# A hybrid retention and attention layer: the MLP norm's weight applied per channel block, a fixed order in the first q and k panels, and the embedding's products in the other PSUM pool

## The chip, the cores and the metric

The kernel runs on one core of a Trainium2 chip. The metric is the device time of one execution in microseconds (us), as the median of several runs. The engines of the core work side by side, each through its own queue in order: TensorE (PE) multiplies, VectorE (DVE) and ScalarE (ACT) work on tiles, GpSimd (POOL) does a few small things, SyncE (SP) starts most transfers. Products are added up in PSUM, in banks of 128 partitions x 512 numbers (fp32); everything else lies in SBUF.

## The reference

One layer on 512 tokens (S) of 1024 channels (D); everything is fp32. The MLP has 4096 hidden channels. What matters here:

```
rmsnorm(x, g) = x * rsqrt(mean(x*x) + eps) * g
h  = rmsnorm(x, g_mix);  z = h @ w_in        # retention q, k, v, gate; attention q, k, v; merge gates
x  = x + (sig(gA) * (A @ w_ret_out) + sig(gB) * (B @ w_att_out)) @ w_o
x  = x + relu(rmsnorm(x, g_mlp) @ w_up)**2 @ w_down
x  = x + sig(rmsnorm(x, g_ple) @ w_ple_gate) * (p @ w_ple_proj)
```

A is the retention, B the attention of three groups of four heads, whose q and k are normed per head and rotated (rotary).

## The kernel before, in words

**Products.** Each fp32 operand is split into a high part, rounded to the matmul's type, and a low part, the rest. A product is three matmuls (mm3, L235 to L241): high x high, high x low, low x high, each of 128x128 by 128x512. A piece of weights (raw, 256 rows x 512 columns, 512 KB) is fetched through SP and split by split_unit: whi by a copy on ACT (L227), wlo by a subtraction on DVE (L228). `ahead` and `AHEAD` set how many pieces are split before they are used. There are two PSUM pools of four banks: psg (names pg) and psa (names pt, pa, pb, ph and others).

**Turning.** The operand that a product contracts over must lie with channels on the partitions. split_T (L308) turns a half of a token tile (128 tokens x 512 channels) by four transposes on PE (L315) into one bank, and then makes the high and low parts from the bank. Without a weight this is one copy on ACT (L328) and one subtraction on DVE (L329), 128x512 each. With a weight (gcol) it is done for each of the four 128-channel blocks: the channel is now the partition, so that the weight is a scale of one number per partition in ACT's copy (L323) and in DVE's combined multiply and subtract (L324). The retention's output is turned in this way.

**Start (setup, first_panel).** setup starts the transfers on SP in order: the columns of x and of the first weights by turns (L390, L391), x by tokens (L397, 4 x 512 KB), then the rotation tables and gains (load_tables), then the next weights. A table of weights per channel, gcol (40 columns), comes through ACT's queue (L382). PE does WARM = 10 matmuls on zeros (L408). first_panel (L438) multiplies the q columns of attention group 0; its scaling and splitting is pinned into a fixed order. token_factors (L502) squares x by tokens on ACT (L508) and makes the norm's factors. For each of four token tiles att_proj squares the product per head (L578), makes a factor on DVE (L579) and POOL (L580), rotates (four operations on DVE, L531 to L536, with the tables C and S of L560), and scales (L585). Then follows the k panel in the same manner with rows_gemm.

**w_o and the embedding (tail).** The product with w_o is one level of Strassen-like recursion with seven products (seven_gemm, L943). Its sums go from PSUM into x on DVE (acc, L967); one pair of sums passes through a tile m (copied by ACT, L981, added to on DVE, L995). Whenever a half of a token tile of x is complete, `ready` (in tail) calls gain_T (L357): a multiplication with g_mlp as a row table gr on DVE (L362), then, some steps later, split_T without a weight into h2h and h2l, the operand of w_up. `later` and `tick` place such steps between products: the lag is a number of ticks. mean_squares (L366) squares x on ACT for the MLP norm's factors, with the lag 3 + 2j. Then embed (L490) multiplies p with w_ple_proj: 8 banks of 6 matmuls, copied out by ACT and DVE in turns (L145, L149) and stored. Its banks are psg's, in which seven_gemm also has the sums that are still to be added to x. seven_gemm and embed are under manual_schedule for ACT and DVE: their order on these two is that of the code. PE's order is made by a scheduler.

Of the kernel before, what the change touches and what calls it, by code (L numbers as in the profile page):

```python
# [31 lines left out]
WARM = 10  # L32
# [43 lines left out]
class Block:  # L76
# [140 lines left out]
    def split_unit(self, raw, g0):  # L217

        nc = self.nc
        k = raw.shape[1]  # L220
        hi = self.wsp.tile([P, 1024], F32, tag="whi", name=self.nm("whi")).rearrange("p (k n) -> p k n", k=k)
        lo = self.wsp.tile([P, 1024], F32, tag="wlo", name=self.nm("wlo")).rearrange("p (k n) -> p k n", k=k)
        if g0 is None:
            for i in range(k) if self.pinned else [slice(0, k)]:
                if self.hook is not None:
                    self.hook(i)
                self.pin(nc.scalar.activation(R(hi[:, i]), raw[:, i], AF.Copy))  # L227
                nc.vector.tensor_tensor(R(lo[:, i]), raw[:, i], hi[:, i], op=ALU.subtract)  # L228
# [14 lines left out]
    def rows_gemm(self, act, nk, consume, perm=False, group=2, need=None, halves=False):  # L243
# [3 lines left out]
        for u0 in range(0, nu, group):  # L247
            us = self.units(min(group, nu - u0))
            for t in range(NT):
                if need is not None:  # L250
                    need(t, u0)
                if u0 == 0:
                    banks[t] = self.gbank()
# [54 lines left out]
    def split_T(self, src, t, gcol, c, dst, bank=None):  # L308

        nc = self.nc  # L310
        for part in src:
# [4 lines left out]
            for k in range(n):  # L316
# [6 lines left out]
                nc.scalar.activation(R(hi), i, AF.Copy, scale=g)  # L323
# [24 lines left out]
    def gain_row(self, name):  # L348
        out = []
        for h in range(2):  # L350
            g = self.a[name][0]
            t = self.tabp.tile([P, 512], F32, tag="tab", name=self.nm("gr"))
            self.nc.sync.dma_start(t, bass.AP(tensor=g.tensor, offset=g.offset + 512 * h, ap=[[0, P], [1, 512]]))
            out.append(t)
        return out

    def gain_T(self, x, t, h, gain, dst, key, lag, bank=None):  # L357

        y = x[:, h * 512 : (h + 1) * 512]
        if gain is not None:  # L360
            y = self.tmp("y")
            self.nc.vector.tensor_tensor(y, x[:, h * 512 : (h + 1) * 512], gain[h], op=ALU.mult)  # L362
        self.later(lag, lambda: self.split_T([y], t, None, 4 * h, dst, bank), (key, t, h))
# [15 lines left out]
    def setup(self):  # L379
        nc, a = self.nc, self.a  # L380
        self.gcol = self.const.tile([P, 40], F32, name="gcol")
        nc.scalar.dma_start(self.gcol, a["vec_cols"])  # L382
# [16 lines left out]
        self.load_tables()  # L399
# [38 lines left out]
    def first_panel(self, consume):  # L438
# [23 lines left out]
        for k in range(KD // 2):  # L462
            for t in range(NT):
                part(t, k)
        self.pinned = True
        self.token_factors()
        self.pinned = False
        for t in range(NT):
# [3 lines left out]
            if t == 0:  # L472
# [17 lines left out]
    def embed(self):  # L490
# [3 lines left out]
        for half in range(2):  # L494
# [5 lines left out]
            self.rows_gemm(([hi], [lo]), 2, store)  # L500

    def token_factors(self):  # L502

        nc = self.nc
        ss = self.small(NT, "ss")
        for t in range(NT):
            j = self.big("j").rearrange("p a b -> p (a b)")[:, :D] if t == 0 else j
            self.pin(nc.scalar.activation(j, self.x_tiles[t], AF.Square, accum_out=ss[:, t : t + 1]))  # L508
# [58 lines left out]
    def att_proj(self, g, n):  # L567
# [3 lines left out]
        rots = []  # L571

        def consume(t, ps):
            ss, v, r = self.small(H, "ss"), self.small(H, "v"), self.small(H, "r")
            j = self.tmp("j")
            for h in range(H):
                c = slice(h * HD, (h + 1) * HD)
                nc.scalar.activation(j[:, c], ps[:, c], AF.Square, accum_out=ss[:, h : h + 1])  # L578
            nc.vector.tensor_scalar(v, ss, 1.0 / HD, self.floor[:, t : t + 1], op0=ALU.mult, op1=ALU.add)  # L579
            nc.gpsimd.tensor_tensor(r, v, self.mhalf[:, :H], op=ALU.pow)  # L580
            if not tabs:
                tabs.append(self.tables(g, n))
            C, Sn = tabs[0]
            o = self.rotate(ps, C[:, t], Sn[:, t])
            nc.vector.tensor_tensor(o.rearrange("p (h e) -> p h e", h=H), o.rearrange("p (h e) -> p h e", h=H),  # L585
                                    r.unsqueeze(2).to_broadcast([P, H, HD]), op=ALU.mult)
            rots.append(o)

        if lazy:
            self.first_panel(consume)  # L590
# [34 lines left out]
    def attention(self, g):  # L625
        nc = self.nc
        qT = self.att_proj(g, 0)
        if g == 0:
            self.load_rest()
        kT = self.att_proj(g, 1)  # L630
# [380 lines left out]
    def tail(self, mx):  # L1011
        nc, a = self.nc, self.a
        xs = self.xs
        g2 = self.gain_row("g_mlp")
# [11 lines left out]
        def ready(t, j, free):  # L1026
# [3 lines left out]
            self.gain_T(xs[t], t, j, g2, h2, "h2", 2 * j if late else 1 + t // 2,  # L1030
                        None if late else (lambda s: free) if t < 2 else self.gbank)
# [16 lines left out]
        for f in range(NF // 2):  # L1048
# [21 lines left out]
            if f == NF // 2 - 1:  # L1070
# [3 lines left out]
                def ready(t, j, free):  # L1074
                    late = (t < 2) == (j == 0)
                    self.gain_T(xs[t], t, j, None, h3, "h3", 0 if late else 1 + t // 2,
# [69 lines left out]
_INS = ["x", "w_in", "g_mlp", "w_ret_out", "w_att_out", "w_o", "w_up", "w_down", "w_ple_proj", "w_ple_gate"]  # L1146
# [25 lines left out]
```

## Time and profile before

| | us |
|---|---|
| Three runs | 1007.2, 1004.25, 1005.76 |
| Median | 1005.76 |
| The profiled execution | 1004.37 |
| Its span in the trace | 1002.5 |
| Between the two | 1.9 |
| PE busy | 990.5 |
| DVE busy | 639.6 |
| ACT busy | 446.6 |

In rows of the trace stand the start in us from the span's start, the duration, the engine, the line, the operation, output<-inputs by the program's names, partitions x elements, and the count; in brackets the idle time ahead of it and what ended it. Consecutive instructions on an engine overlap by a tenth of a us or so, so that the time from start to start is shorter than the duration. In a table of groups, busy time and mean ns stand behind the first bar, and idle time ahead of the group and who ended it behind the second.

### The profile page before, as it was taken

What the parts mean: (1) busy time and instruction counts of PE and PEld (TensorE: products, weight loads), DVE (VectorE), ACT (ScalarE), POOL (GpSimd) and SP (SyncE); (2) the same over time, 40 slices, a digit from 0 to 9 for tenths busy, and PEclk for the clock granted to TensorE, in tenths of its full rate; (3) what the DMA queues carried; (4) which work ended last, traced back from release to release, by engine and by line L of the source; (5) the groups of instructions that cost most, each with busy time, mean ns of one, the idle gap of its engine ahead of it and who ended that gap; (6) DMA issues with size and microseconds to landing.
All of it is one profiled execution on the core that took longest, in us unless ns stands there. A gap on an engine that the chain in (4) does not pass through costs nothing.

```text
span 1002.5 us, 12321 instructions
## 1 busy us (share of the span) xinstructions
PE 990.5 (99%) x4607; PEld 826.8 (82%) x4607; DVE 639.6 (64%) x930; ACT 446.6 (45%) x845; POOL 91.7 (9%) x98
## 2 busy tenths in 40 slices
PE   9899999999999999999999998999999999999998
PEld 6788899889888888888888877888888888888886
DVE  5966675764779345554643698469468658656953
ACT  7435344443534325342422445564454356355451
POOL 1100110110000010001002010101101001010000
PEclk9999999999999999999999999999999999999999
DMA  9622122333254412222446496749748856884911
GB/s 347 241 84 68 61 84 84 106 96 94 66 162 123 122 45 85 85 82 87 133 145 163 128 211 190 207 109 238 190 114 212 222 155 152 226 178 118 313 54 53
DMA packets 89756, 141.14 MB, mean 141 GB/s; under 512 B 6320, under 2 KB 38368, under 8 KB 89696
## 3 DMA queue, kind: packets, MB, share of 16 engines
q1 hardware_dynamic: 78672, 119.36, 36.9%
q0 software_dynamic: 10880, 20.97, 12.5%
q8 instruction: 36, 0.59, 0.2%
q14 instruction: 24, 0.20, 0.1%
q10 hardware_dynamic: 144, 0.02, 0.0%
HBM read 136.09 MB, written 4.24 MB: 140 GB/s over the span
## 4 chain that ended last, share of the span: by engine, by line
PE 93%; DMA 3%; DVE 2%; ACT 1%; issue 1%; SPq 0%; ACTq 0%; DVEq 0%
PE pg L239 26%; PE pg L240 26%; PE pg L241 26%; PE pb L239 3%; PE pb L240 3%; PE pb L241 3%; DMA raw<-in_w_in 2%; PE po L666 1%; PE ph L546 1%; PE pt L315 1%; PE sc L643 1%; DMA x<-in_x 1%; PE ry L846 1%; PE pe L620 1%; PE kv L834 1%
## 5 line engine op out<-in xcount | busy, mean ns | idle before, releaser
L228 DVE TENSOR_TENSOR wlo<-raw,whi 128x1024 fp32r<-128x1024 f32 (+1 forms) x198 | 235.8, 1195 | 119.1 <-ACT whi L227 117.3
L227 ACT ACTIVATE whi<-raw 128x1024 fp32r<-128x1024 f32 (+1 forms) x198 | 203.4, 1033 | 213.7 <-PE pg L241 84.9
L239 PE MATMUL pg<-whi,hh 128*128 128x512 f32 x480 | 198.8, 415 | 2.9 <-DVE ro L534 2.9
L240 PE MATMUL pg<-wlo,hh 128*128 128x512 f32 x480 | 188.1, 392 | 0.1
L241 PE MATMUL pg<-whi,hl 128*128 128x512 f32 x480 | 188.1, 392 | 0.0
L239 PEld LDWEIGHTS pg<-whi,hh 128*128 128x128 f32 x480 | 98.0, 204 | 17.9 <-issue 3.6
L241 PEld LDWEIGHTS pg<-whi,hl 128*128 128x128 f32 x480 | 97.9, 204 | 16.9
L240 PEld LDWEIGHTS pg<-wlo,hh 128*128 128x128 f32 x480 | 98.4, 205 | 14.6 <-DVE wlo L228 0.8
L239 PE MATMUL pg<-h2h,whi 128*128 128x512 f32 x256 | 99.6, 389 | 0.0
L240 PE MATMUL pg<-h2l,whi 128*128 128x512 f32 x256 | 99.6, 389 | 0.0
L241 PE MATMUL pg<-h2h,wlo 128*128 128x512 f32 x256 | 99.6, 389 | 0.0
L196 POOL DMA_DIRECT2D raw<-in_w_down x32 | 38.6, 1206 | 305.8 <-DMA raw<-in_w_down 220.7
L239 PE MATMUL pg<-whi,uh 128*128 128x512 f32 x160 | 62.7, 393 | 0.0
L241 PE MATMUL pg<-whi,ul 128*128 128x512 f32 x160 | 62.5, 392 | 0.0
L240 PE MATMUL pg<-wlo,uh 128*128 128x512 f32 x160 | 62.4, 390 | 0.0
L239 PEld LDWEIGHTS pg<-h2h,whi 128*128 128x128 f32 x256 | 48.0, 188 | 10.1
L241 PEld LDWEIGHTS pg<-h2h,wlo 128*128 128x128 f32 x256 | 48.0, 188 | 10.0
L240 PEld LDWEIGHTS pg<-h2l,whi 128*128 128x128 f32 x256 | 48.0, 188 | 9.9
L239 PE MATMUL pg<-hh,whi 128*128 128x512 f32 x128 | 52.4, 409 | 0.0
L940 DVE TENSOR_TENSOR ul<-z,uh 128x1792 fp32r<-128x1792 f32 x20 | 40.5, 2026 | 15.5 <-ACT uh L939 15.5
L241 PE MATMUL pg<-hh,wlo 128*128 128x512 f32 x128 | 50.0, 390 | 0.0
L240 PE MATMUL pg<-hl,whi 128*128 128x512 f32 x128 | 49.9, 390 | 0.0
(196 smaller groups left out, 1615.8 us busy)
## 6 DMA issues: line engine op xcount, KB each, us to landing
raw<-in_w_in SPq DMA_DIRECT2D x72, 512.0 KB, 3.9
raw<-in_w_down SPq DMA_DIRECT2D x48, 512.0 KB, 4.4
raw<-in_w_up SPq DMA_DIRECT2D x32, 512.0 KB, 5.4
raw<-in_w_down POOLq DMA_DIRECT2D x32, 512.0 KB, 6.0
raw<-in_w_o SPq DMA_DIRECT2D x12, 512.0 KB, 3.8
x<-in_x SPq DMA_DIRECT2D x8, 512.0 KB, 6.1
raw<-in_w_ret_out SPq DMA_DIRECT2D x8, 512.0 KB, 3.5
raw<-in_w_o POOLq DMA_DIRECT2D x8, 512.0 KB, 5.9
```

Of the source, the lines that this page charges most:

```text
L196: self.nc.gpsimd.dma_start(raw, rows(add[0]), accum_op=ALU.add)
L227: self.pin(nc.scalar.activation(R(hi[:, i]), raw[:, i], AF.Copy))
L228: nc.vector.tensor_tensor(R(lo[:, i]), raw[:, i], hi[:, i], op=ALU.subtract)
L239: t.matmul(ps, sh, mh, start=first, stop=False, skip_group_check=more)
L240: t.matmul(ps, sh, ml, start=False, stop=False, skip_group_check=more)
L241: t.matmul(ps, sl, mh, start=False, stop=last, skip_group_check=more)
L315: nc.tensor.transpose(ps[:, k * P : (k + 1) * P], part[:, k * P : (k + 1) * P], self.ident)
L546: self.nc.tensor.transpose(ps[:, t * P : (t + 1) * P], rots[t][:, h * HD : (h + 1) * HD], self.ident)
L620: self.nc.tensor.transpose(ps[:, k * P : (k + 1) * P], e[:, k * P : (k + 1) * P], self.ident)
L643: nc.tensor.matmul(sc[:, h * P : (h + 1) * P], qT[:, h, rs], kT[:, h, rs], start=True, stop=True)
L666: nc.tensor.matmul(po[:, h * P : (h + 1) * P], v[:, vt, h * HD : (h + 1) * HD], pt, start=b == 0, stop=b == len(blocks) - 1)
L940: nc.vector.tensor_tensor(R(lo), src, hi, op=ALU.subtract)
```

## The change

1. **g_mlp per channel.** gcol has 48 columns, the last eight with g_mlp. The row table gr, its two transfers and the multiplication L362 are gone; split_T gets the weight as gcol, and so does four ACT and four DVE operations of 128x128 for each of eight halves.
2. **Pool.** embed takes its banks from psa.
3. **Lag.** mean_squares has lag 9.
4. **First q and k panels.** They are under manual_schedule for ACT and DVE. The tables C and S are made ahead of the squares of x; a tile is rotated ahead of its factor and scaled one tile later; the next weights are split after tile 1 instead of tile 0.
5. **Start.** The tables' transfers stand ahead of x. The first half of the first weights goes through ACT's queue, ahead of gcol, and is split by a copy on DVE; the first twelve matmuls stand in another order; WARM is 7.

```
-WARM = 10
+WARM = 7
...
+                early = self.hook is not None and i == 0 and not self.loaded
+                if early:
+                    self.tc.keep_in_program_order(nc.vector.tensor_copy(R(hi[:, i]), raw[:, i]))
...
-    def gain_T(self, x, t, h, gain, dst, key, lag, bank=None):
-
-        y = x[:, h * 512 : (h + 1) * 512]
-        if gain is not None:
-            y = self.tmp("y")
-            self.nc.vector.tensor_tensor(y, x[:, h * 512 : (h + 1) * 512], gain[h], op=ALU.mult)
-        self.later(lag, lambda: self.split_T([y], t, None, 4 * h, dst, bank), (key, t, h))
+    def half_T(self, x, t, h, gain, dst, key, lag, bank=None):
+
+        self.later(lag, lambda: self.split_T([x[:, h * 512 : (h + 1) * 512]], t, gain, 4 * h, dst, bank), (key, t, h))
...
-                nc.sync.dma_start(raw[:, k], src[k * P : (k + 1) * P])
+                queue = nc.sync if u or k else nc.scalar
+                queue.dma_start(raw[:, k], src[k * P : (k + 1) * P])
+                if queue is nc.scalar:
+                    nc.scalar.dma_start(self.gcol, a["vec_cols"])
             self.raws.append((raw, None))
+        self.load_tables()
         self.x_tiles = []
...
-        self.load_tables()
         self.fetch(6)
...
-        for k in range(KD // 2):
+        (wh, wl), mm = us[0], nc.tensor.matmul
+        parts = [self.stat(self.hT, 0, t, False) for t in range(NT)]
+        for t, (sh, _) in enumerate(parts):
+            mm(banks[t], sh, wh[:, 0], start=True, stop=False)
+        for t, (_, sl) in enumerate(parts):
+            mm(banks[t], sl, wh[:, 0], start=False, stop=False)
+        for t, (sh, _) in enumerate(parts):
+            mm(banks[t], sh, wl[:, 0], start=False, stop=False)
+        for k in range(1, KD // 2):
             for t in range(NT):
                 part(t, k)
-        self.pinned = True
-        self.token_factors()
-        self.pinned = False
+        tables()
+        self.token_squares()
...
-            if t == 0:
+            if t == 1:
                 self.pinned = True
                 self.ahead(2)
...
-            self.rows_gemm(([hi], [lo]), 2, store)
+            self.rows_gemm(([hi], [lo]), 2, store, bank=self.bank)
...
+            C, Sn = tabs[0]
+            rots.append(self.rotate(ps, C[:, t], Sn[:, t]))
+            if lazy and t == 0:
+                self.token_factors()
             nc.vector.tensor_scalar(v, ss, 1.0 / HD, self.floor[:, t : t + 1], op0=ALU.mult, op1=ALU.add)
             nc.gpsimd.tensor_tensor(r, v, self.mhalf[:, :H], op=ALU.pow)
...
+            if t:
+                scale(t - 1)
+            factors.append(r)
+            if t == NT - 1:
+                scale(t)
...
-        g2 = self.gain_row("g_mlp")
+        g2 = lambda k: self.gcol[:, 40 + k : 41 + k]
...
-                self.later(3 + 2 * j, lambda: self.mean_squares(xs[t], v2[:, t : t + 1]), ("v2", t))
+                self.later(9, lambda: self.mean_squares(xs[t], v2[:, t : t + 1]), ("v2", t))
```

Line numbers move a little: whi and wlo are L231 and L232 after the change, the blocks L327 and L328, acc L980, the addition to m L1008, the rotation L535 to L540, the scale L597.

The order of the instructions, as the two programs have it, at three places. On DVE in the w_o product, before: x is the residual, y its product with the weight gr, wlo a weight's low part, h2l the low part of w_up's operand.

```order
L967 SCALAR_TENSOR_TENSOR x_4442<-pg_4800,one,x_4442 128x512
L967 SCALAR_TENSOR_TENSOR x_4442<-pb_4820,one,x_4442 128x512
L362 TENSOR_TENSOR y_4897<-x_4442,gr_4746 128x512
L228 TENSOR_TENSOR wlo_4900<-raw_4845,whi_4899 128x1024
L329 TENSOR_TENSOR h2l_4890<-pb_4881,h2h_4888 128x4x128
L329 TENSOR_TENSOR h2l_4890<-pb_4882,h2h_4888 128x4x128
L228 TENSOR_TENSOR wlo_4931<-raw_4927,whi_4930 128x1024
L967 SCALAR_TENSOR_TENSOR x_4443<-pg_4772,one,x_4443 128x512
L362 TENSOR_TENSOR y_4947<-x_4443,gr_4744 128x512
```

And after, with the same four sums into x ahead:

```order
L980 SCALAR_TENSOR_TENSOR x_4442<-pg_4789,one,x_4442 128x512
L980 SCALAR_TENSOR_TENSOR x_4442<-pb_4809,one,x_4442 128x512
L980 SCALAR_TENSOR_TENSOR x_4442<-pg_4796,one,x_4442 128x512
L980 SCALAR_TENSOR_TENSOR x_4442<-pb_4816,one,x_4442 128x512
L232 TENSOR_TENSOR wlo_4892<-raw_4841,whi_4891 128x1024
L328 SCALAR_TENSOR_TENSOR h2l_4886<-pb_4877,gcol,h2h_4884 128x128 x4
L328 SCALAR_TENSOR_TENSOR h2l_4886<-pb_4878,gcol,h2h_4884 128x128 x4
L232 TENSOR_TENSOR wlo_4935<-raw_4931,whi_4934 128x1024
L980 SCALAR_TENSOR_TENSOR x_4443<-pg_4768,one,x_4443 128x512 x2
L980 SCALAR_TENSOR_TENSOR x_4443<-pg_4775,one,x_4443 128x512
```

The multiplications are gone, and between the two wlo stand 2 x 4 blocks that read the banks pb and ACT's h2h in place of 2 operations. On ACT at the same place, before (m is the tile of one pair of sums, whi a weight's high part, pT the turned p):

```order
L981 ACTIVATE m_4883<-pg_4772 128x512
L981 ACTIVATE m_4893<-pg_4779 128x512
L227 ACTIVATE whi_4899<-raw_4845 128x1024
L328 ACTIVATE h2h_4888<-pb_4881 128x4x128
L328 ACTIVATE h2h_4888<-pb_4882 128x4x128
L227 ACTIVATE whi_4930<-raw_4927 128x1024
L487 ACTIVATE pT_4748<-praw_4749 128x1024
```

And after:

```order
L994 ACTIVATE m_4879<-pg_4768 128x512
L994 ACTIVATE m_4887<-pg_4775 128x512
L231 ACTIVATE whi_4891<-raw_4841 128x1024
L327 ACTIVATE h2h_4884<-pb_4877,gcol 128x128 x4
L327 ACTIVATE h2h_4884<-pb_4878,gcol 128x128 x4
L231 ACTIVATE whi_4934<-raw_4931 128x1024
L487 ACTIVATE pT_4744<-praw_4745 128x1024
```

The weights' high parts stand behind 4 or 8 blocks, where they stood behind 1 or 2 operations. On PE, the embedding's products with the turned p in after; the matmuls with h2h and h2l are w_up's first, and x is what is turned:

```order
L243 MATMUL pa_5140<-whi_5061,pT_4744 128x512
L244 MATMUL pa_5140<-wlo_5062,pT_4744 128x512
L245 MATMUL pa_5140<-whi_5061,pT_4744 128x512
L243 MATMUL pg_5285<-h2h_4883,whi_5126 128x512
L244 MATMUL pg_5285<-h2l_4885,whi_5126 128x512
L243 MATMUL pg_5286<-h2h_4883,whi_5126 128x512
L244 MATMUL pg_5286<-h2l_4885,whi_5126 128x512
L319 MATMUL pt_5150<-ident,x_4443 128x128 x4
L243 MATMUL pa_5163<-whi_5061,pT_4744 128x512
L244 MATMUL pa_5163<-wlo_5062,pT_4744 128x512
L245 MATMUL pa_5163<-whi_5061,pT_4744 128x512
L243 MATMUL pa_5163<-whi_5061,pT_4744 128x512
```

In before all 48 products of the embedding, in banks pg, stand ahead of w_up's first; now 36 of them stand behind w_up's first, which needs whi_5126 from ACT and the blocks of h2h and h2l.

On DVE in the head, before: ss are sums of squares, ro the rotated tiles, wlo_290 the first half of the k panel's weights.

```order
L511 TENSOR_SCALAR v_245<-ss_239 128x4
L513 TENSOR_SCALAR floor<-v_245 128x4
L579 TENSOR_SCALAR v_268<-ss_267,floor 128x4
L560 TENSOR_TENSOR C_277<-rotc_114,mg_115 128x512
L560 TENSOR_TENSOR S_278<-rotc_114,mg_115 128x512
L531 TENSOR_TENSOR ro_281<-pg_187,C_277 128x512
L534 TENSOR_TENSOR ro_282<-pg_187,S_278 128x4x64 x2
L228 TENSOR_TENSOR wlo_290<-raw_118,whi_289 128x512
L536 TENSOR_TENSOR ro_283<-ro_281,ro_282 128x512
L228 TENSOR_TENSOR wlo_290<-raw_118,whi_289 128x512
```

And after, where wlo_318 is that weight:

```order
L535 TENSOR_TENSOR ro_268<-pg_186,C_238 128x512
L538 TENSOR_TENSOR ro_269<-pg_186,S_239 128x4x64 x2
L540 TENSOR_TENSOR ro_270<-ro_268,ro_269 128x512
L515 TENSOR_SCALAR v_275<-ss_242 128x4
L517 TENSOR_SCALAR floor<-v_275 128x4
L587 TENSOR_SCALAR v_261<-ss_260,floor 128x4
L535 TENSOR_TENSOR ro_307<-pg_187,C_238 128x512
L538 TENSOR_TENSOR ro_308<-pg_187,S_239 128x4x64 x2
L540 TENSOR_TENSOR ro_309<-ro_307,ro_308 128x512
L587 TENSOR_SCALAR v_300<-ss_299,floor 128x4
L597 TENSOR_TENSOR ro_270<-ro_270,r_262 128x512
L232 TENSOR_TENSOR wlo_318<-raw_118,whi_317 128x512 x2
```

The first wlo of the k panel stood behind the first steps of one tile's rotation, and stands behind two whole tiles and one scale now; C and S stand ahead of these rows.

More of the change, by code (lines that the diff above doesn't have):

```diff
@@ L252, in rows_gemm @@
                 if u0 == 0:
-                    banks[t] = self.gbank()
+                    banks[t] = (bank or self.gbank)()
                 cols = [slice(0, 512)] if not (halves and t == NT - 1) else [slice(0, 256), slice(256, 512)]
@@ L380, in setup @@
         nc, a = self.nc, self.a
[L381 to L382 removed]
+        self.gcol = self.const.tile([P, 48], F32, name="gcol")
         xr = [self.big("xr") for _ in range(2)]
@@ L1143, in run @@
         assert self.used == len(self.plan) and not self.queue
-_INS = ["x", "w_in", "g_mlp", "w_ret_out", "w_att_out", "w_o", "w_up", "w_down", "w_ple_proj", "w_ple_gate"]
+_INS = ["x", "w_in", "w_ret_out", "w_att_out", "w_o", "w_up", "w_down", "w_ple_proj", "w_ple_gate"]
 def kernel(**inputs):
```

55 lines of the change are left out of this document (25 added, 30 removed).

## The prediction

> **What bounds the kernel now.** I read the page's first part, then the chain of waits of PE, then the two stretches that the change touches, the w_o product with the embedding (583 to 623 us) and the first panels (0 to 53 us). PE is the bound.
>
> ```profile
> span 1002.5 us, 12321 instructions
> PE 990.5 (99%) x4607; PEld 826.8 (82%) x4607; DVE 639.6 (64%) x930; ACT 446.6 (45%) x845; POOL 91.7 (9%) x98
> ```
>
> So only some 12 us of the span are not matmuls, and a change can gain no more than PE's waits. These are all of them that have a releaser:
>
> ```profile
> PE pg L239 <- DVE ro L534: 2.9, 1, 2.9
> PE pg L239 <- DVE x L967: 2.1, 1, 2.1
> PE warm L408 <- DVE warm L404: 1.5, 1, 1.5
> PE pg L240 <- DVE wlo L228: 0.5, 1, 0.5
> PE ph L546 <- DVE ro L536: 0.2, 1, 0.2
> ```
>
> Each is a wait for DVE. The first is in the head (at 34 us), the second and fourth are in the embedding's products. The places that the change touches hold these three, 5.5 us together. To lose is easier than to gain: an average of 64% hides that DVE is full just where the change adds work. In the table of windows the columns are length, then busy time and count of PE, PEld, DVE, ACT, POOL:
>
> ```profile
> 583.20:609.30 26.10, 25.51 (x122) 19.96 (x120) 25.58 (x35) 9.89 (x13) 2.42 (x2) 1.00 0.72 189
> 609.30:623.20 13.90, 11.80 (x55) 9.46 (x56) 12.33 (x21) 11.47 (x26) 0.00 (x0) 1.00 0.61 187
> ```
>
> In the w_o product DVE is busy 25.58 of 26.10 us and PE waits almost never: both are full. What is put into DVE's queue here, work or waiting, comes out at the end.
>
> **Part 1, the weight per channel block.** Groups of 583.2 to 624 us:
>
> ```profile
> L228 DVE TENSOR_TENSOR wlo<-raw,whi 128x1024 fp32r<-128x1024 f32 x11 | 13.4, 1220 | 0.1
> L362 DVE TENSOR_TENSOR y<-x,gr 128x512 f32<-128x512 f32 x8 | 5.5, 692 | 0.3
> L329 DVE TENSOR_TENSOR h2l<-pt,h2h 128x512 fp32r<-128x512 f32 x6 | 4.0, 682 | 0.0
> L329 DVE TENSOR_TENSOR h2l<-pb,h2h 128x512 fp32r<-128x512 f32 x2 | 1.3, 683 | 0.0
> ```
>
> Removed from DVE: 8 multiplies L362 (5.5 us) and 8 splits L329 (4.0 + 1.3), 10.8 us. Added: 32 blocks of 128x128 on ACT, then 32 on DVE. The same lines of split_T run in the retention, and show what such a block costs (timeline of ACT and of DVE):
>
> ```profile
> 382.10 0.37 ACT L323 ACTIVATE A<-pt,gcol 128x128 fp32r<-128x128 f32 x1 [0.46 <-PE pt L315]
> 382.89 0.37 ACT L323 ACTIVATE A<-pt,gcol 128x128 fp32r<-128x128 f32 x1 [0.42 <-DVE A L324]
> ...
> 390.93 0.61 ACT L323 ACTIVATE A<-pt,gcol 128x128 fp32r<-128x128 f32 x2
> ```
> ```profile
> 382.50 0.35 DVE L324 SCALAR_TENSOR_TENSOR A<-pt,gcol,A 128x128 fp32r<-128x128 f32 x1 [0.47 <-ACT A L323]
> 383.29 0.35 DVE L324 SCALAR_TENSOR_TENSOR A<-pt,gcol,A 128x128 fp32r<-128x128 f32 x1 [0.43 <-ACT A L323]
> ```
>
> By busy time it is even: 32 x 0.35 = 11.2 for 10.8. But DVE's block waits for ACT's, and ACT's second block of the same bank waits for DVE's first (0.42 <-DVE A L324). The period is 382.89 - 382.10 = 0.79 us, in which DVE works 0.35. Only blocks of two banks in turn go without that wait (0.61 for two, at 390.93), and the change issues the four blocks of a bank one after another. Four cost DVE 0.35 + 3 x 0.79 = 2.72 us where a split and a multiply cost 1.36, and the period holds ACT as well, where the next whi stands behind the blocks, and DVE's next wlo behind that whi. To price this I follow DVE's queue in its new order. The pitches, from rows of this stretch:
>
> ```profile
> 600.00 0.68 DVE L995 TENSOR_TENSOR m<-m,pb 128x512 f32<-128x512 f32 x1
> 600.71 1.42 DVE L967 SCALAR_TENSOR_TENSOR x<-m,one,x 128x512 f32<-128x512 f32 x2
> 602.04 0.68 DVE L995 TENSOR_TENSOR m<-m,pb 128x512 f32<-128x512 f32 x1
> ...
> 608.01 1.22 DVE L228 TENSOR_TENSOR wlo<-raw,whi 128x1024 fp32r<-128x1024 f32 x1
> 609.14 1.28 DVE L329 TENSOR_TENSOR h2l<-pt,h2h 128x512 fp32r<-128x512 f32 x2
> ```
> ```profile
> 598.13 2.00 ACT L227 ACTIVATE whi<-raw 128x1024 fp32r<-128x1024 f32 x2
> ```
>
> From start to next start an addition into x (acc, L967) takes 0.67, an addition to m 0.71, a wlo 1.13; a whi 0.95 on ACT. Time t runs from the first acc of the stage to the first matmul of w_up:
>
> ```profile
> 583.23 0.74 DVE L967 SCALAR_TENSOR_TENSOR x<-pg,one,x 128x512 f32<-128x512 f32 x1
> ...
> 623.16 0.39 PE L239 MATMUL pg<-h2h,whi 128*128 128x512 f32 x1
> ```
>
> This took 39.9 us. After the change, ends on DVE: 4 accs 2.7; wlo 3.8; four blocks 6.5 (3.8 + 2.72); four of the second bank 9.2; ACT, free at 8.9, makes the whi until 9.8, so that the wlo waits and ends at 10.9; 3 accs, the split of p (at wlo's pitch), an acc 14.7; wlo 15.9; four blocks 18.6; again a wlo behind the whi behind the blocks (18.3 + 0.95) 20.4; four blocks 23.1; 2 additions to m and 4 accs 27.2; wlo 28.3; 2 accs 29.7; wlo 30.8; eight blocks 36.2. ACT, held by the same eight until 35.9, makes two whi until 37.8, and the second one is for w_up, whose first products now stand among the embedding's: PE stops there until 37.9. From there PE has 36 of the embedding's 48 matmuls, 14 of w_up and 8 transposes before the place that answers to 623.16:
>
> ```profile
> 594.95 0.39 PE L239 MATMUL pb<-whi,uh 128*128 128x512 f32 x1
> ...
> 597.00 0.60 PE L315 MATMUL pt<-ident,y 128*128 128x128 f32 x4
> 597.36 0.48 PE L239 MATMUL pb<-whi,uh 128*128 128x512 f32 x1
> 597.67 0.39 PE L240 MATMUL pb<-wlo,uh 128*128 128x512 f32 x1
> ```
>
> Nine matmuls from 594.95 to 597.00 give 0.228 each; four transposes take 597.67 - 597.00 - 0.23 = 0.44. So 50 x 0.228 + 0.9 = 12.3, t = 50.2; the 14 of w_up (3.2) are work done early, 47.0 remain: **+7.1 us** on 39.9. Who waits, by PE's own count: for the wlo at 20.4 about 1 us, for the wlo at 28.3 about 5 us, 1 us more for x of the two accs (29.7) ahead of the transposes, and 3 us at 37.9.
>
> A rule bears on the 5 us. What the trace shows of the granted clock: PE's longest wait is 2.86 us (row at 36.97 below), and PEclk is 1.00 in both windows above. The Trainium skill, TensorE: Matmul & The Clock Gate, section "What's actually happening", says that an idle window of about 3.4 us returns PE to half rate, until it was busy for such a window again. No run here shows it. By that rule the 23 matmuls behind this wait run at half rate, and the sum becomes +8.5 (the third rival).
>
> **Part 2, the other pool.** With psa's banks the embedding no longer waits until accs free psg's: the 2.1 us go. What is late next is the row above, 37.9 for ACT and DVE, so the term is nothing by itself and is contained in the 7.1. It is worth its 2.1 only if part 1 is free. **Part 3, mean_squares later:** 4 pairs of ACT squares leave the embedding for w_up, where ACT and DVE are idle for most of the time; nothing, since PE is busy throughout and the factors are only needed at w_down's sums:
>
> ```profile
> 623.20:640.00 16.80, 16.80 (x76) 13.92 (x75) 5.61 (x10) 6.63 (x13) 2.42 (x2) 1.00 0.97 283
> ```
>
> **Part 4 and 5, the head.** The transfers run at the limit, and the tables are put ahead of x:
>
> ```profile
> 10.00:20.00 10.00, 10.00 (x46) 8.29 (x45) 6.31 (x10) 8.78 (x15) 0.00 (x0) 1.00 1.04 398
> ```
> ```profile
> rotc<-in_c_rot SPq DMA_DIRECT2D x2, 512.0 KB, 9.6
> mg<-in_rot_gains SPq DMA_DIRECT2D x1, 256.0 KB, 8.6
> ```
>
> 768 KB, 786 thousand bytes, at 398 GB/s are 2.0 us by which x comes later. Rows of the head, DVE, then PE, then a window:
>
> ```profile
> 22.29 0.23 DVE L579 TENSOR_SCALAR v<-ss,floor 128x4 f32<-128x4 f32 x1 [0.65 <-ACT j L578]
> ...
> 35.48 0.68 DVE L531 TENSOR_TENSOR ro<-pg,C 128x512 f32<-128x512 f32 x1
> ...
> 38.26 0.22 DVE L579 TENSOR_SCALAR v<-ss,floor 128x4 f32<-128x4 f32 x1
> ```
> ```profile
> 36.97 0.47 PE L239 MATMUL pg<-whi,hh 128*128 128x512 f32 x1 [2.86 <-DVE ro L534]
> ...
> 52.50 0.60 PE L546 MATMUL ph<-ident,ro 128*128 128x128 f32 x4
> ```
> ```profile
> 36.97:52.50 15.53, 15.53 (x68) 12.78 (x69) 15.01 (x29) 6.61 (x27) 3.46 (x4) 1.00 0.57 204
> ```
>
> At 22.29 ACT was through with the squares of x and of tile 0, which stand behind them; with x 2.0 later that is 24.3. Tile 0's rotate reads the same bank after those squares, so DVE begins with it then (C and S are ready, as the new order has it). One tile's rotate, scale and small steps take 38.26 - 35.48 = 2.8. Ahead of the first wlo of the k panel DVE now has two tiles less one scale (as large as L531, 0.7), and token_factors' two small steps (0.2 each): 24.3 + 5.6 - 0.7 + 0.4 = 29.6, the wlo's half (128x512) 0.7: 30.3. PE can start two matmuls earlier with whi alone, and has 94 left, 21.4 us: 51.7 against 52.50, **-0.8 us**. The wait of 2.9 us becomes a wait for that wlo. The faster start (first weights on ACT's queue, split by DVE, 12 matmuls regrouped, WARM 7) gains under 1 us that ends in the same wait, so nothing. Bounds: the whole 2.9 gained, if the wlo is not late; +0.9, if the third tile's rotate is late too. The gcol column costs 8 numbers per partition, and two transfers of 256 KB go; neither is waited for.
>
> **Sum.** 7.1 - 0.8 = +6.3 us. The profiled execution took 1004.37 us, 1.4 under the median of the runs shown (1005.76), and would take 1010.7; the median 1012.1. About 0.3%, 3 us, is what a measurement of this kernel tells from no change.
>
> **The rivals.** *Gain.* The blocks overlap and DVE keeps pace. Then the waits of 2.1 and 0.5 go and the head's 0.8: 1005.76 - 3.4 = 1002.4. The turning point: 10.8 us over 32 blocks, a period of 0.34. For it speaks the 0.61 for two at 390.93; against it 0.79, with the same function and the same order in a bank. 0.14. *No change.* Only DVE waits for ACT, since in the retention ACT's wait may be one for the output tile: a period of 0.37 from ACT's row, 32 x 0.37 - 10.8 = +1.0, which eats what slack there is and leaves no gain from the pool: 1005.76 + 1.0 - 0.8 = 1006.0. Against it: the change's blocks share one output tile (h2h) just as the retention's share A, so that such a wait would be here too. 0.14. *Slower by more.* The granted clock falls to half for the 23 matmuls between the 5 us wait and the one at 37.9: they take 5.2 us more (23 x 0.228), of which that wait hides 3, so 1012.1 + 2.2 = 1014.3. For it: no wait in the trace is as long; against it: after the 2.86 us ahead of 36.97 the matmuls up to 52.50 are not slowed (68 in 15.53 us, 0.228 each, in the last window above). 0.15. *The forecast,* 0.57. It is also its own mechanism on the slow side: it decides as soon as the period is over 0.34 plus what slack DVE has, 0.5 of 26.1 us.
>
> Faster by over 0.3%: 0.14; within: 0.14; slower: 0.72. The range leaves out most of the gain, and reaches to the clock case with the head's +0.9: 1003 to 1015.5.
>
> **What would show it.** Right: the waits for ro L534 and for x L967 are gone; in their place waits for wlo (L232) of about 5 us near the end of the w_o product, 2 to 3 us before the first product with h2, and 1 to 2 us for the first wlo of the k panel, before 30 us; L327 and L328 at a period near 0.79, with idle of DVE put down to ACT h2h. Wrong: L328's idle is near nothing, and 583 to 623 us has shrunk; or PEclk falls below 1.00 after the long wait; or the first k panel starts without a wait.

## The result and the profile after

| | median, us | ratio to before | 95% interval |
|---|---|---|---|
| before (5 runs, 1004.25 to 1007.45) | 1007.2 | | |
| after (5 runs, 1011.38 to 1012.7) | 1011.75 | 1.0057 | 1.0046 to 1.0069 |

The change makes the kernel slower by 0.57%. That ratio and its interval are estimated from the runs of both kernels; the quotient of the two medians would be 1.0045, since before's five runs lie up to 3.2 us apart. In the trace of after the span is 1009.9 us, 7.4 more than before. The page's first rows:

```profile
span 1009.9 us, 12354 instructions
PE 993.6 (98%) x4604; PEld 828.9 (82%) x4604; DVE 639.5 (63%) x947; ACT 451.0 (45%) x868; POOL 98.1 (10%) x98
```

DVE's total work is the same to 0.1 us; what changed is when it can be done. PE's waits in after (total, times, longest):

```profile
PE pg L244 <- DVE wlo L232: 4.5, 2, 3.9
PE pg L243 <- ACT whi L231: 2.4, 3, 1.4
PE pg L458 <- ACT hh L439: 1.8, 1, 1.8
...
PE pb L243 <- DVE h2l L328: 0.7, 1, 0.7
```

The waits for ro L534 (2.9) and for x L967 (2.1) are gone. In their place stand 7.6 us for wlo, whi and h2l, all of them in the w_o product and the embedding, and 1.8 us ahead of the first real matmul. Three groups, from the sums' start to the first plain stretch of w_up (582.8 to 633 us); behind the second bar is the idle time and who ended it:

```profile
L327 ACT ACTIVATE h2h<-pt,gcol 128x128 fp32r<-128x128 f32 x24 | 8.6, 367 | 20.8 <-DVE h2l L328 12.3 <-PE pt L319 8.5
L328 DVE SCALAR_TENSOR_TENSOR h2l<-pt,gcol,h2h 128x128 fp32r<-128x128 f32 x24 | 8.3, 349 | 7.8 <-ACT h2h L327 7.8
L328 DVE SCALAR_TENSOR_TENSOR h2l<-pb,gcol,h2h 128x128 fp32r<-128x128 f32 x8 | 2.7, 349 | 2.6 <-ACT h2h L327 2.6
```

DVE works 11.0 us on the 32 blocks and stands idle 10.4 us among them, waiting for ACT, which itself waited for DVE. On DVE's timeline the blocks come at the retention's period, 0.78 to 0.79 us:

```profile
587.07 0.35 DVE L328 SCALAR_TENSOR_TENSOR h2l<-pb,gcol,h2h 128x128 fp32r<-128x128 f32 x1
587.85 0.35 DVE L328 SCALAR_TENSOR_TENSOR h2l<-pb,gcol,h2h 128x128 fp32r<-128x128 f32 x1 [0.44 <-ACT h2h L327]
588.64 0.35 DVE L328 SCALAR_TENSOR_TENSOR h2l<-pb,gcol,h2h 128x128 fp32r<-128x128 f32 x1 [0.43 <-ACT h2h L327]
589.42 0.61 DVE L328 SCALAR_TENSOR_TENSOR h2l<-pb,gcol,h2h 128x128 fp32r<-128x128 f32 x2 [0.43 <-ACT h2h L327]
...
592.98 1.23 DVE L232 TENSOR_TENSOR wlo<-raw,whi 128x1024 fp32r<-128x1024 f32 x1 [0.59 <-ACT whi L231]
```
```profile
589.02 0.62 ACT L327 ACTIVATE h2h<-pb,gcol 128x128 fp32r<-128x128 f32 x2 [0.42 <-DVE h2l L328]
```

The last row on DVE is the wlo that waits for a whi which stood behind the blocks on ACT. The rows with x2 are the fourth block of one bank and the first of the next: neither engine waits between them, although all eight blocks go into the same pair of tiles, h2h and h2l. So the wait goes with the bank that both engines read, and not with the output tile. On PE the two long waits, the place that answers to 623.16 before, and the windows around the first wait (the third number from the right is the granted clock, behind the busy times):

```profile
611.45 0.80 PE L244 MATMUL pg<-wlo,uh 128*128 128x512 f32 x1 [3.93 <-DVE wlo L232]
612.11 1.97 PE L319 MATMUL pt<-ident,x 128*128 128x128 f32 x8
...
620.64 0.50 PE L243 MATMUL pg<-h2h,whi 128*128 128x512 f32 x1 [1.42 <-ACT whi L231]
...
633.10 0.39 PE L243 MATMUL pg<-h2h,whi 128*128 128x512 f32 x1
```
```profile
582.90:609.00 26.10, 22.41 (x101) 16.70 (x99) 19.41 (x35) 12.09 (x23) 2.42 (x2) 1.00 0.64 168
...
611.40:615.00 3.60, 3.55 (x13) 2.94 (x14) 3.06 (x5) 0.81 (x3) 0.00 (x0) 0.54 0.49 148
```

In the stretch where before had PE busy for 25.51 and DVE for 25.58 of 26.1 us, both now have holes: 22.41 and 19.41. And after the wait of 3.93 us the granted clock is 0.54 for some 3 us: eight transposes take 1.6 us (612.11 to 613.74), where four took 0.44 before.

The first sum into x stands at 582.90 in after and at 583.23 before, so the head gave 0.33 us. From there to 633.10 are 50.2 us; less 14 matmuls of w_up done early (3.2) that is 47.0 against 39.9: +7.1. From then on PE stays 6.8 us behind its old time to its last matmul; the rest of the 7.4 is in the end of the span behind PE.

### The profile page after: what moved, and what is told of

Same layout as the page of the kernel before. It is cut to its first block, busy times and chain, and to the rows that moved or that the text cites. A ratio compares the mean times of both kernels' runs of the same rounds, so it can differ in the third digit from the quotient of the medians.

```text
span 1009.9 us, 12354 instructions
## 1 busy us (share of the span) xinstructions
PE 993.6 (98%) x4604; PEld 828.9 (82%) x4604; DVE 639.5 (63%) x947; ACT 451.0 (45%) x868; POOL 98.1 (10%) x98
## 3 DMA queue, kind: packets, MB, share of 16 engines
q1 hardware_dynamic: 78240, 118.57, 36.2%
## 4 chain that ended last, share of the span: by engine, by line
PE 94%; DVE 3%; ACT 1%; issue 1%; DMA 0%; ACTq 0%; DVEq 0%
PE pg L243 26%; PE pg L245 26%; PE pg L244 26%; PE pb L245 2%; PE pb L244 2%; PE pb L243 2%; PE po L679 1%; PE ph L550 1%; PE sc L656 1%; PE pt L319 1%; DVE h2l L328 1%; DVE wlo L232 1%; PE ry L859 1%; PE pe L630 1%; DVE x L980 1%
## 5 line engine op out<-in xcount | busy, mean ns | idle before, releaser
L232 DVE TENSOR_TENSOR wlo<-raw,whi 128x1024 fp32r<-128x1024 f32 (+1 forms) x198 | 235.4, 1195 | 117.2 <-ACT whi L231 115.5
L231 ACT ACTIVATE whi<-raw 128x1024 fp32r<-128x1024 f32 (+1 forms) x197 | 202.4, 1036 | 205.4 <-PE pg L245 77.5
L243 PE MATMUL pg<-whi,hh 128*128 128x512 f32 x476 | 196.6, 414 | 0.1
```

The source lines that it names most:

```text
L243: t.matmul(ps, sh, mh, start=first, stop=False, skip_group_check=more)
```

## The experiments

The theory: ACT and DVE take turns on the four blocks of a bank, DVE was full in the w_o product, and the idle time in these turns delays its whole queue there. The main rivals: the operations' number and size, the embedding's other pool with w_up's products pulled ahead, the late start of the head. Every run had its times beside runs of before on the same chip (median 1005.6 to 1005.7).

**Tail alone (e1_tail_only).** Before with parts 1 to 3; of the change's diff the head is left out:

```
+        g2 = lambda k: self.gcol[:, 40 + k : 41 + k]
...
+            self.rows_gemm(([hi], [lo]), 2, store, bank=self.bank)
...
+                self.later(9, lambda: self.mean_squares(xs[t], v2[:, t : t + 1]), ("v2", t))
```

> The kernel before with parts 1 to 3 alone (weight per channel block, the embedding's other pool, the later mean squares); the head is that of before. Theory (the blocks' alternation of ACT and DVE in the w_o product makes the loss, the head gives 0.3 us of gain in the trace): 7 us over before, ratio 1.007, PE's wait for ro L534 of 2.9 us is back, and the waits of about 4 us for a wlo and 1.4 us for a whi are in the w_o product. Rival (the loss is in the head, whose first matmul starts 1.4 us later in the changed kernel): the ratio is 1.000 to 1.003.

Measured: 1013.24 us, ratio 1.0073 (1.0059 to 1.0086). PE's waits are again 4.5 us for wlo, 1.7 for whi, 0.7 for h2l, and 2.2 for ro L521 (the old L534). The whole loss is in the tail; the head of the change, rather, gives something back. Part of that is the clock, which falls in e1 behind the head's wait of 2.2 us (last section).

**Row table again (e2_rows_back).** The changed kernel without part 1:

```
-        g2 = lambda k: self.gcol[:, 40 + k : 41 + k]
+        g2 = self.gain_row("g_mlp")
...
-            self.half_T(xs[t], t, j, g2, h2, "h2", ...
+            self.gain_T(xs[t], t, j, g2, h2, "h2", ...
```

> The changed kernel with part 1 undone alone: g_mlp is again a row table that DVE multiplies with, and a half is split by one ACT and one DVE operation; pool, lag and head are those of the change. Theory: the loss goes wholly, and now the other pool is worth its 2.1 us and the wait for wlo of 0.5 us goes too: 2 to 3 us faster than before, ratio 0.997 to 0.998. Rival (the loss comes from the embedding's other pool, which lets w_up's first products stand ahead of the embedding's and wait there): a loss of 3 us or more is left, ratio 1.003 or more.

Measured: 1002.98 us, ratio 0.9975 (0.9965 to 0.9984). As the theory has it: parts 2 to 5 gain 0.25%, and part 1 turns that into a loss of 0.57%. The rival with the pool is out: w_up's first products stand ahead in this run too.

**The operations of a bank apart (e3_apart).** In split_T, for the eight halves of the w_o product, four ACT operations, then four DVE operations:

```
                 self.pin(nc.scalar.activation(R(hi), i, AF.Copy, scale=g))
-                nc.vector.scalar_tensor_tensor(R(lo), i, g, hi, op0=ALU.mult, op1=ALU.subtract)
+                if not self.apart:
+                    nc.vector.scalar_tensor_tensor(R(lo), i, g, hi, op0=ALU.mult, op1=ALU.subtract)
+            for k in range(n if self.apart and gcol is not None else 0):
+                ...
+                nc.vector.scalar_tensor_tensor(R(lo), i, gcol(kk), hi, op0=ALU.mult, op1=ALU.subtract)
```

> The changed kernel, in which the four ACT operations of a bank are issued first and the four DVE operations after them, in the w_o product alone. The number and the size of the operations stay; only the wait of ACT's second to fourth block for DVE's block before it is gone. Theory (the cost is that alternation): four blocks take DVE about 1.1 us (4 x 0.26 from the 0.61 for two) instead of 2.7, DVE has 32 x 0.27 = 8.6 us where before had 10.8; the 4 us wait goes; the time is 2 to 3 us under before, ratio 0.997 to 0.998. Rival (the cost is that of 64 small operations for 16 larger ones): the ratio stays 1.004 or more.

Measured: 1000.38 us, ratio 0.9948 (0.9934 to 0.9961), 11 us under the changed kernel with the same operations. On DVE eight blocks now stand in one row, and PE's two windows are full:

```profile
586.77 2.15 DVE L336 SCALAR_TENSOR_TENSOR h2l<-pb,gcol,h2h 128x128 fp32r<-128x128 f32 x8
588.84 1.22 DVE L232 TENSOR_TENSOR wlo<-raw,whi 128x1024 fp32r<-128x1024 f32 x1
```
```profile
582.60:609.00 26.40, 26.40 (x129) 21.66 (x128) 25.56 (x49) 14.90 (x33) 2.42 (x2) 1.00 0.74 203
609.00:625.00 16.00, 16.00 (x76) 13.14 (x75) 12.20 (x26) 12.70 (x33) 0.00 (x0) 1.00 0.76 251
```

Eight blocks take 2.07 us from start to next start, 0.26 each, where four took 2.7 in after. The cost was the turns, not the number or size. PE's order of some 50 matmuls in this stretch differs from after's as well, since its scheduler sees other readiness; the run can't part that from the waits' end, but no wait of PE is left in the tail. It gained more than the 2 to 3 us expected. In part that is because before lost more than its named waits there: at two places between 583 and 623 us its PE started 0.3 and 0.4 us late without one. In part it is the clock, which falls in most runs of before behind the head's wait (see the sum, below), a wait that e3 does not have.

**gcol first (e4_gcol_first).** One transfer moved:

```
+        nc.scalar.dma_start(self.gcol, a["vec_cols"])
...
-                if queue is nc.scalar:
-                    nc.scalar.dma_start(self.gcol, a["vec_cols"])
```

> The changed kernel with one transfer moved: the table gcol stands ahead of the first half of the weights on ACT's queue again. Theory (in the head the first wlo of the k panel at 30.6 us decides, not the start): the first matmul comes about 1.4 us earlier, at 5 us, PE then waits about 1.5 us for that wlo, and the time is that of the changed kernel within 0.3 us in the trace. Rival (the late start is what is lost in the head): 1.4 us faster than the changed kernel, with no new wait.

Measured: 1011.39 us, ratio 1.0061 (1.0048 to 1.0075), the changed kernel's time. But not by the expected way: the first matmul comes at 5.59 us (after: 6.47), and no wait for the wlo shows. The reason is in the pace of the first twelve matmuls, here in after:

```profile
6.47 2.07 PE L458 MATMUL pg<-whi,hh 128*128 128x512 f32 x4 [1.84 <-ACT hh L439]
8.34 1.91 PE L460 MATMUL pg<-whi,hl 128*128 128x512 f32 x4
10.04 1.34 PE L462 MATMUL pg<-wlo,hh 128*128 128x512 f32 x4
11.22 0.39 PE L243 MATMUL pg<-whi,hh 128*128 128x512 f32 x1
```

The first eight are 0.43 to 0.47 us apart, the pace of the warm matmuls (3.17 us for seven), the last four 0.30, and only from 11.2 on it is 0.23; in e4 the twelve take from 5.59 to 10.81. So PE reaches the k panel at about 30 us with or without gcol first (30.27 in after, 29.86 in e4). The expected wait stayed away, but so did the rival's 1.4 us.

**Pool alone (e5_only_pool).** Before with part 2:

```
-            self.rows_gemm(([hi], [lo]), 2, store)
+            self.rows_gemm(([hi], [lo]), 2, store, bank=self.bank)
```

> The kernel before with part 2 alone: the embedding's banks from psa. Theory (the 2.1 us wait for x L967 is a wait for a bank of psg, and nothing else is late at that place when DVE has the work of before): the wait goes, 2 us under before, ratio 0.998, and no new wait of over 1 us in the w_o product and the embedding. Rival (what is late next is DVE again, so that part 2 is worth nothing by itself): ratio 1.000, a wait for wlo or y of some 2 us in its place.

Measured: 1006.66 us, ratio 1.0006 (0.9997 to 1.0015). My theory fell here. The wait for a bank is gone, and another of the same size stands in its place. So the rival's time came, though not by the wait that it named (wlo or y):

```profile
613.82 0.50 PE L239 MATMUL pg<-h2h,whi 128*128 128x512 f32 x1 [2.05 <-ACT whi L227]
```

On ACT that whi (612.73) stands behind four squares of mean_squares (610.28 to 612.7), and on DVE the two last sums into x (613.12) behind a step that waits for these squares:

```profile
612.14 0.62 ACT L370 ACTIVATE j<-x 128x512 f32<-128x512 f32 x1
612.66 0.19 ACT L370 ACTIVATION_READ_ACCUMULATOR j<-x 128x1 f32 x1
612.75 1.04 ACT L227 ACTIVATE whi<-raw 128x1024 fp32r<-128x1024 f32 x1
```
```profile
612.88 0.16 DVE L372 TENSOR_TENSOR s<-ss 128x1 f32<-128x1 f32 x1 [0.88 <-ACT j L370]
613.08 0.15 DVE L373 TENSOR_SCALAR v<-s 128x1 f32<-128x1 f32 x1
613.15 0.74 DVE L967 SCALAR_TENSOR_TENSOR x<-pg,one,x 128x512 f32<-128x512 f32 x1
```

These rows are from before, where the same squares lie at the same place; I had read its 2.1 us as a wait for a bank.

**Part 1 apart, alone (e6_only_apart).** Before with part 1 and the loop of e3:

```
-        g2 = self.gain_row("g_mlp")
+        g2 = lambda k: self.gcol[:, 40 + k : 41 + k]
...
-            self.AHEAD = 3
+            self.AHEAD, self.apart = 3, True
```

> The kernel before with part 1 alone, the four ACT operations of a bank issued ahead of the four DVE operations; pool, lag and head are those of before. Theory (DVE is the bound of the w_o product and now has 8.6 us where it had 10.8): the sums into x are 2 us earlier, so the bank waits of 2.1 and 0.5 us nearly go even without the other pool: 2 to 2.5 us under before, ratio 0.9975 to 0.998; PE's wait of 2.9 us in the head stays. Rival (the gain of the run with the operations apart came from the pool, the weight per block gives nothing): ratio 0.999 to 1.000.

Measured: 1006.35 us, ratio 0.9999 (0.999 to 1.0007). The sums come at 612.14 against 613.15, still behind the same step (idle 0.87 for ACT j), while PE is 1.4 us earlier at the embedding and waits 2.6 us for them; and behind that wait it is slow:

```profile
612.94 1.12 PE L317 MATMUL pt<-ident,x 128*128 128x128 f32 x4 [2.59 <-DVE x L962]
613.71 0.78 PE L239 MATMUL pg<-whi,pT 128*128 128x512 f32 x1
614.28 0.63 PE L240 MATMUL pg<-wlo,pT 128*128 128x512 f32 x1
614.71 0.63 PE L241 MATMUL pg<-whi,pT 128*128 128x512 f32 x1
```

From 613.71 to 615.56 the matmuls are 0.43 to 0.57 apart, which takes the last of the gain. So the theory lacked a term: the squares hold up the end of the w_o product, whatever else is faster.

**Head of the change, mended (e7_apart_warm10).** e3 with gcol first and WARM 10.

```
-WARM = 7
+WARM = 10
```

> The run with the operations apart in the w_o product (1000.38 us), with gcol ahead of the first weights on ACT's queue and WARM at 10 again. Theory (the change starts 2.5 us late: 1.4 for gcol, and its first twelve matmuls are 0.43 us apart instead of 0.23, since PE stood still for 1.8 us after seven warm ones; but the first wlo of the k panel at 30.3 us would be waited for anyway): the twelve are 0.23 to 0.3 apart, PE waits about 2 us for that wlo, and the time stays within 0.5 us of 1000.4. Rival (the late start is a loss in full): 998, ratio 0.992 to 0.993 to before.

Measured: 999.93 us, ratio 0.994 (0.9928 to 0.9953). Eight of the twelve matmuls are 0.23 apart now, the first four still 0.41; PE waits 0.8 us for the wlo, not 2. The time is within the expected 0.5 us, and the rival (998) is out.

**And x ahead of the tables (e8_apart_xfirst).** As e7, with this:

```
-        self.load_tables()
         self.x_tiles = []
...
             self.x_tiles.append(v)
+        self.load_tables()
         self.fetch(6)
```

> As the run before it (operations apart, gcol first, WARM 10), and the transfers of x stand ahead of the tables again. Theory (the head is bound by x, its squares, two tiles' rotation and the first wlo of the k panel): x comes 2 us earlier, the rotation of tile 0 starts when the tables have landed at 22.4 us and C and S are made (1.2), at 23.6 instead of 24.7: 1 us less than the run before it, ratio to before 0.9935 to 0.994. Rival (the tables have to be early, for DVE makes C and S while it waits for x): no gain, or 1 us more.

Measured: 998.86 us, ratio 0.9928 (0.9914 to 0.9942), 1.1 us less than e7. DVE's first row of the rotation stands at 22.87 (e7: 23.68) and the k panel's last matmul ends 0.8 us earlier. This is the fastest version found, 0.72% under before and 1.3% under the change. The tables' place ahead of x, as the change has it, costs about 1 us.

**Lag alone (e9_only_lag).** Before with part 3:

```
-                self.later(3 + 2 * j, lambda: self.mean_squares(xs[t], v2[:, t : t + 1]), ("v2", t))
+                self.later(9, lambda: self.mean_squares(xs[t], v2[:, t : t + 1]), ("v2", t))
```

> The kernel before with part 3 alone: mean_squares nine ticks later, so that in DVE's queue the last two sums into x no longer stand behind a step that waits for ACT's squares. PE's order is that of before. Theory (the squares, not the pool, hold up the end of the w_o product: the sums begin at 611.6 instead of 613.15 us): PE's wait of 2.1 us shrinks to about 0.6, 1.5 us under before, ratio 0.9985. Rival (the squares have room, and the lag gives nothing, as the prediction had it): ratio 1.000, the 2.1 us stay.

Measured: 1004.22 us, ratio 0.9985 (0.9976 to 0.9994), as expected, and PE's order is that of before. The wait of 2.1 is now

```profile
PE pg L239 <- DVE x L967: 0.5, 1, 0.5
```

**Pool and lag (e10_pool_lag).** Before with the lines of e5 and e9.

> The kernel before with parts 2 and 3. Theory (the other pool alone gave nothing because ACT's whi for w_up then stood behind the same squares; with both, sums and whi come early): the waits of 2.1 us for x and for whi are both gone, 2 us under before, ratio 0.998. Rival (the other pool has w_up's first products wait for DVE in any case): 1.000.

Measured: 1004.57 us, ratio 0.9986 (0.9977 to 0.9995). Both 2.1 us waits are gone, as expected, and waits of 0.5, 0.4 and 0.4 us for wlo and y are left; but the gain is no more than that of the lag alone. So the other pool adds nothing measurable to the lag while DVE has the multiplications.

**Part 1 apart, and lag (e11_apart_lag).** Before with the edits of e6 and e9.

> The kernel before with part 1, its ACT operations ahead of its DVE operations, and part 3, without the other pool. Theory (the run without the lag had DVE 1.4 us earlier, but the sums behind the wait for the squares): the sums come at 610.7 instead of 612.1 us, PE's wait of 2.6 us for x shrinks to about 1, and the time is 1.5 us under before, ratio 0.9985; all of the gain only comes with the pool. Rival: 1.000 as without the lag, or 0.9975 and below, if the pool isn't needed at all.

Measured: 1003.7 us, ratio 0.9979 (0.997 to 0.9988). The interval holds both the theory's 0.9985 and the rival's 0.9975; the wait for x is 1.1 us, as the theory has it. Weight and lag together give 0.2% without the pool. e3, which has the pool and the change's head besides, stands at 0.9948. The head by itself was worth 0.0011 (e10 to e2) and 0.0016 (e1 to after), beside other tails; so some 0.15 to 0.2% is left for the pool once the operations are apart. That is an estimate by differences: no run has the pool as its only change there.

**The fastest with early squares (e12_best_early_squares).** e8 with the lag back:

```
-                self.later(9, lambda: self.mean_squares(xs[t], v2[:, t : t + 1]), ("v2", t))
+                self.later(3 + 2 * j, lambda: self.mean_squares(xs[t], v2[:, t : t + 1]), ("v2", t))
```

> The fastest run so far (operations apart, gcol first, WARM 10, x ahead of the tables; 998.86 us) with the lag of mean_squares back at 3 + 2j. Theory (the squares stand ahead of the last sums and of w_up's whi again): about 2 us are lost, 1000.5 to 1001, ratio 0.9945 to 0.995, with a wait of 1 to 2 us for whi or x near 613 us. Rival (with DVE's work cut by a fifth there is room for them): 998.9, ratio 0.993.

Measured: 1001.2 us, ratio 0.9959 (0.9946 to 0.9971), 2.3 us over e8, a little more than expected. The wait is back where the theory puts it:

```profile
PE pg L243 <- ACT whi L231: 2.0, 1, 2.0
```

## Why the prediction was right, and where it was not

The prediction was 1012.1 us (1003 to 1015.5), slower; measured 1011.75. Two of the signs that it named for being wrong came true all the same: the granted clock fell after the long wait, and the first k panel starts without a wait. The time held because neither of them set it: the end of the tail hung on the queues of DVE and ACT, and the head's term was small. By its steps:

- *The bound, and DVE full in the w_o product:* right. With 10.4 us of idle time among DVE's blocks, PE was through with the stage 7.1 us later.
- *Part 1, +7.1:* right as a sum and nearly at every stop. DVE's wlo, due at t = 28.3, ended at 611.31 (28.4), the two sums after it at 29.7 (due 29.7), the eight blocks at 36.2 (36.2); PE went on at 37.7 (37.9). The cause is shown by e3, in which the turns are taken away and the operations stay. PE's waits were forecast as 1, 5, 1 and 3 us, and were 0.9 (0.38 and 0.53), 4.5 (0.62 and 3.93), none and 1.4; a wait of 0.7 for h2l was not forecast. The last was shorter because PE itself came later, by the clock.
- *The clock, as a rival:* the mechanism came, and its price did not. The granted clock fell after the wait of 3.93 us, as the rule of the Trainium skill that stood beside that rival has it (TensorE: Matmul & The Clock Gate, section "What's actually happening"). But it was back when PE's second matmul after the transposes had passed (614.74), not after 23 matmuls, and what was lost (3.3 us from 611.45 on for three matmuls and eight transposes that need 1.6) lay wholly within the wait that ended at 620.64. I had let it last over everything up to that wait, which the rule as I quoted it does not say: by it the slow stretch ends after some 3.4 us of work, and 23 matmuls at half pace (0.456 each) are 10.5 us. The measured 3.3 us agree with that part of the rule, and the rival's price was a misreading of it.
- *Part 2, "worth its 2.1 only if part 1 is free", and part 3, "nothing":* wrong, both. The pool is worth nothing alone (e5), and as long as DVE has the multiplications it adds nothing to the lag (e10); only with the operations apart does it seem to be worth something (see e11). The lag is worth 0.15% alone (e9) and 0.3% in the fastest version (e12 over e8). The failed step is my reading of the row of before in which PE waits for x L967: I asked which bank was late, and not why DVE was late with that sum. Its own row, with the step ahead of it that waits 0.88 us for ACT's squares, would have told. Neither changed the forecast, since part 1 covered them.
- *Part 5, "gains under 1 us that ends in the same wait":* of the wrong sign. gcol, behind 256 KB on the same queue, came 2 us later than before (first hh at 5.69, before 3.74), and PE's first matmul at 6.47 instead of 5.03; and the twelve took 4.75 us (6.47 to 11.22), 2.0 more than at 0.228. Together PE came to the k panel some 2.9 us later (its 13th matmul at 11.22 instead of 8.30).

```profile
5.69 1.34 ACT L439 ACTIVATE hh<-xr,gcol 128x512 fp32r<-128x512 f32 x2 [2.53 <-DMA gcol<-in_vec_cols]
```

- *The head, -0.8:* -0.3 (52.20 against 52.50). The first wlo was forecast for 30.3 and stands at 29.93 to 30.6, so that term was 0.3 short. The step that was too small is x's delay: ACT's squares of x begin at 18.55 instead of 16.16, 2.4 us later where I had 2.0. PE came to the wlo just then by itself, and the wait of 1 to 2 us for it that I named isn't there. e4, e7 and e8 show both limits: taking away the late start alone gives 0.4 us between the medians, and x in front of the tables another 1.1.
- *The sum:* +6.3 forecast, +6.8 at PE's last matmul, of which 7.1 and -0.3. The whole span grew by 7.4, and by the ratio the change costs only 5.7, since the trace of before is one of its quicker executions. Of 27 runs of before, 5 had a mean granted clock of 0.999 or more and took 1003.84 to 1004.57 us, as the profiled one; 22 had 0.997 or 0.998 and took 1005.46 to 1007.25. The clock's fall after the head's wait, below, is the likely reason: of the traces with this head, e1, e9 and e10 (mean clock 0.995 to 0.998) show the fall there; before, e5 and e11 (0.999) do not, nor does e6, whose fall comes in the tail. After has no such wait in the head. So that the forecast median came within 0.4 us is in part luck: the loss in the trace was some 1 us larger than forecast, and most runs of before lose some 1.4 us that its one trace does not show.

```profile
52.20 0.60 PE L550 MATMUL ph<-ident,ro 128*128 128x128 f32 x4
```

## What to carry to other kernels

Where two engines read one bank, operation by operation in turns, the order of issue decides: in this kernel, where DVE was full, the same 64 operations cost 11 us more as pairs than as four and four. Ask of each wait why the releaser was late, and follow its queue one step further, to the small step ahead of it that waits for a third engine; the other pool (e5) and the cheaper blocks (e6) gained nothing as long as that step stood there. Where an engine is full in one stage, work it out there, stop by stop in the new order; the average of 64% says nothing.

## What the runs showed of the hardware

The granted clock falls after shorter waits than I thought, and with a delay. In e1 PE waited 2.19 us, ran four matmuls at full pace and then slowed down:

```profile
36.95 0.47 PE L239 MATMUL pg<-whi,hh 128*128 128x512 f32 x1 [2.19 <-DVE ro L521]
37.26 0.40 PE L240 MATMUL pg<-wlo,hh 128*128 128x512 f32 x1
37.49 0.39 PE L241 MATMUL pg<-whi,hl 128*128 128x512 f32 x1
37.72 0.39 PE L239 MATMUL pg<-whi,hh 128*128 128x512 f32 x1
37.95 0.56 PE L240 MATMUL pg<-wlo,hh 128*128 128x512 f32 x1
```

In e9 the same happened behind a wait of 2.5 us, for eight matmuls 0.43 apart, and a window shows the granted clock; before had a wait of 2.86 us and no fall in its trace:

```profile
36.90:42.00 5.10, 4.88 (x15) 3.88 (x16) 4.82 (x11) 0.00 (x0) 1.01 (x1) 0.67 0.25 68
```

So a wait of 2 to 3 us may or may not cost another 1.6 us (in e1 nine matmuls from 37.95 on take 3.64 us instead of 2.05). The Trainium skill (TensorE: Matmul & The Clock Gate, section "What's actually happening") has the clock fall after an idle window of some 3.4 us, in a window that runs freely; the free window would fit the chance in it, the length does not: here 2.2 us were enough. In the head the first eight matmuls of after ran 0.43 to 0.47 us apart, as slowly as those of e1 behind its wait, while the profile's clock column reads 1.00 from 6 to 10 us, in after as in e4. Whether the column misses a low clock there or something else slows these matmuls, the runs do not tell; the pace is read from the spacing.
